# The last group of a second MLP stage by plain products in place of a seven-product scheme

## The chip, the cores and the metric

The kernel runs on one core of a Trainium2 chip. The metric is the device time in microseconds (us) of one execution; lower is better. Inputs and outputs are float32.

## The reference, cut to what matters

The reference is one decoder block: a mixer (dilated attention beside a gated MLP), then a squared-ReLU MLP. The change lies in the second matrix product of that MLP and in the normalisation behind it:

```
h = _rmsnorm(x, norm_pre_mlp)                    # x: (2048, 1024)
a = relu(einsum('bsd,df->bsf', h, w_mlp_in))     # (2048, 4096)
y = einsum('bsf,fd->bsd', a * a, w_mlp_out)      # (2048, 1024)
x = x + _rmsnorm(y, norm_post_mlp)
```

## The kernel before, in words

**Precision.** Every float32 operand of a matmul is split into a high part (a rounded copy made by ScalarE, line L70) and a low part (the source minus the high part, line L78, on VectorE or GpSimd). A product is then three matmuls: high by high, high by low, low by high. Every matmul of this stage takes a 128x128 stationary tile of the squared activations S and a 128x512 moving tile of the weights W2, and adds up in a PSUM bank of 128x512 float32.

**The scheme of the second stage.** The 2048 rows are cut into 16 row tiles of 128, taken two by two: a "block" is a pair of row tiles, `ci` 0 and 1, and there are 8 blocks (two halves of the sequence, `i` = 0 to 3 in each). The 1024 output columns are two halves, `nh` 0 and 1. The inner dimension of 4096 is 32 slices of 128; two slices form a `q`, two `q` a group `g`, so there are 8 groups of four slices. A "step" is one block in one group: 64 steps, numbered `n`, all 8 blocks of group 0 first, then group 1, and so on. The last group is the steps 56 to 63 (`FIRST_END` is 56, `FINAL` is 63).

For a step and a `q`, S is a 2x2 matrix of tiles (row tile by slice) and W2 a 2x2 matrix (slice by column half: B11, B12, B21, B22). The four output tiles need eight tile products done plainly. The kernel uses Winograd's form of Strassen's scheme instead, with seven (`yproduct`, numbered 1 to 7): sums of S tiles and of W2 tiles are formed first (`sum_s` on GpSimd, L1331 to L1334; `sum_w2` and `sum_w2_last` on GpSimd, L1284 to L1292; the sums of weights are named T1 to T4), and several products add to more than one output. Products 1, 6, 7 and 4 grow in one PSUM bank ("ya" in the profile): after each of them VectorE reads the bank and adds it to one output in SBUF (L1537), and only then may TensorE add the next product into the same bank. Product 2 has a bank of its own ("yb"), products 5 and 3 share one ("yc"). So a step has 7 x 2 x 3 = 42 matmuls and seven evictions by VectorE. The output of each step is collected over the groups in SBUF tiles `acc` (the profile shows them under the names of the buffers that they reuse: acc_yt, acc_gmlp, B_acc, acc_y, acc_xr).

**Plain steps.** `plain(n, k)`, with `k` from 0 to 7, does the eight products directly. Output `k // 2` takes two terms, `k` even and `k` odd, side by side in one bank ("y", L1514): B11 and B21 for the left column half, B12 and B22 for the right. VectorE evicts after the second term (L1518). A plain step has 8 x 2 x 3 = 48 matmuls and four evictions. Before the change, three steps are plain: 59, 61 and 63 (the list `PLAIN`). They need B12 as it was, but `sum_w2` has overwritten it in place, so the columns of B12 are loaded again (two DMAs of 256 KB into `w2r_b`) and split again on ScalarE and VectorE.

**Order.** TensorE's order is written out by hand: the list `yorder` sorts all products by a place `t0 + t`, where `t0` grows by 7 with each step. A seven-product step n has its products at 0 (1), 3 (2), 4 (6), 8 (7), 9 (5), 12 (4) and 13 (3), so its last four lie among the first three of step n+1: TensorE does other products while VectorE reads the shared bank. The other engines work in the order of the program text, which follows the same loop; each has one queue, worked off in order. `at(k, gen)` puts a piece of work behind the k-th product of the list. The sums and splits of S for step n+3 (`sum_s`) follow the last product of step n, in pieces; the splits of W2 for the next group (`ops_of`, `op_w2`) follow products 1, 2, 6, 7, 5 and 4 of the last step of a group, when the spot that they overwrite is free, their low parts on GpSimd.

**The end of each output.** In the last group each output is final after its last eviction. `end_half` has ScalarE square and sum it (jk, L1458; the junk goes to a PSUM bank) and GpSimd multiply it by the gain `gfin` (L1465). `finish(n)` then forms the reciprocal root on ScalarE and VectorE (`rstd_act`, L119 to L130), and `end` has VectorE compute y * r + x1 (L1471, four of them for each step) and starts the store (L1472); x1 was loaded by `load_x1` on the SP queue. The last step has its own `finish_row`, which ends its two row tiles apart.

**Banks.** All of these, sums and junk alike, take their PSUM bank from `psum_any`, which alternates between two rings of four banks.

Of the kernel before, what the change touches and what calls it, by code (L numbers as in the profile page):

```python
# [8 lines left out]
F32 = mybir.dt.float32  # L9
# [7 lines left out]
P = 128  # L17
# [24 lines left out]
def block_kernel(ctx, tc, a, out):  # L42
    nc = tc.nc
    pe, act, dve, pool, sp = nc.tensor, nc.scalar, nc.vector, nc.gpsimd, nc.sync
    x = a["x"]

    def stack(es, name, bufs=1, side=None, space=None):
        kw = dict(name=name, bufs=bufs, reuse_waits="tile")
        if side:
            kw["side"] = side  # L50
        if space is not None:
            kw["space"] = space
        return es.enter_context(tc.tile_pool(**kw))
# [10 lines left out]
    def psum_aux(name):  # L64
        return ps.tile([P, 512], F32, name=name, tag="aux")

    def split(hi, lo, src, hi_eng="act", lo_eng="dve"):

        if hi_eng == "act":
            act.activation(hi, src, AF.Copy)  # L70
        elif hi_eng == "pool":
            pool.tensor_scalar(hi, src, 1.0, 1.0, op0=OP.mult, op1=OP.mult)  # L72
        else:
            dve.tensor_copy(hi, src)
        if behind_product is not None and lo_eng == "dve":
            behind_product.append((lo, src, f32(hi)))
        else:
            (pool if lo_eng == "pool" else dve).tensor_sub(lo, src, f32(hi))  # L78
# [231 lines left out]
    with ExitStack() as e1a:  # L310
# [6 lines left out]
        for n in range(2):  # L317
            p = psum_aux(f"busy{n}")
# [27 lines left out]
        blocks = [(c, i) for c in range(4) for i in range(4)]  # L346
        qk = [(g, which) for g in range(3) for which in range(2)]
        for half in range(2):
# [15 lines left out]
            for n, (g, which) in enumerate(qk):  # L364
                w = nxt
# [79 lines left out]
    loaded, late, zps = {}, [], {}  # L445
# [246 lines left out]
    for n in range(len(units) + 1):  # L692
        u = None
        if n < len(units):
            g, c, j = units[n]
# [187 lines left out]
    def psum_any(name):  # L883
        cnt[0] += 1
        return ps.tile([P, 512], F32, name=name, tag="mm" if cnt[0] % 2 else "aux")
# [5 lines left out]
    NQ, LEAD, TRAIL = NF // 2, 5, 3  # L891
# [369 lines left out]
    r4 = stack(e3, "r4", 1, side="right")  # L1261
    OPS = ("B11", "B21", "T2", "T3", "T1", "T4", "B22")
    USE = {1: (0, "B11"), 2: (1, "B21"), 6: (2, "T2"), 7: (3, "T3"), 5: (4, "T1"), 4: (5, "T4"), 3: (6, "B22")}
    w2r_, w2_, st_, n_op, spots = {}, {}, {}, [0], []
# [8 lines left out]
    def op_w2(q, name, lo_eng):  # L1273
        w = spots[n_op[0] % 17]
        n_op[0] += 1
        raw = w2r_[q][:, dict(B11=0, B12=1, B21=2, T2=4, T3=1, T1=0, T4=2, B22=3)[name]]
        split(w[:, 0], w[:, 1], raw, "act", lo_eng)
        w2_[q, name] = w
# [10 lines left out]
    def sum_w2_last(q):  # L1289

        r = w2r_[q]
        pool.tensor_sub(r[:, 2], r[:, 2], r[:, 4])  # L1292

    blocks = [(half, i) for half in (first_half, second_half) for i in range(4)]
    ysteps = [(g, half, i) for g in range(NQ // 2) for half, i in blocks]


    PLAIN = [n for n in range(len(ysteps)) if n >= len(ysteps) - len(blocks) and n % len(blocks) in (3, 5, 7)]
    FINAL = len(ysteps) - 1
    OUTPUTS = [(ci, nh) for ci in range(2) for nh in range(2)]  # L1300

# [12 lines left out]
    def sum_s(n):  # L1314
# [6 lines left out]
        st_[n] = w  # L1321
        if n in PLAIN:
            split(w[:, 0, :, :2], w[:, 1, :, :2], raw[:, :, :2], "act", "dve")
# [16 lines left out]
            yield  # L1340

    def ops_of(g, j, lo_eng="pool"):
        for q in (2 * g, 2 * g + 1):
            op_w2(q, OPS[j], lo_eng)

    last_ones = order[n_last:]

# [6 lines left out]
    q = NQ - 1  # L1354
# [76 lines left out]
    FIRST_END = len(ysteps) - len(blocks)  # L1431
    x1_, ss_, y_, wb_, last_rows = {}, {}, {}, {}, {}
# [18 lines left out]
    def end_half(n, ci, h):  # L1451

        g, half, i = ysteps[n]
        if n not in ss_:
            ss_[n] = sm.tile([P, 2, 2], F32, name=f"fs_{n}", tag="fs")
        y = acc[half, i, ci][:, h * 512:(h + 1) * 512]
        junk = psum_any(f"jk_{n}{ci}{h}")
        act.activation(junk, y, AF.Square, accum_out=ss_[n][:, h, ci:ci + 1])  # L1458
        if n == FINAL and h:

            z = acc[blocks[1] + (ci,)][:, :512]
            dve.tensor_mul(z, y, gfin[h])
            y = z
        else:
            pool.tensor_mul(y, y, gfin[h])  # L1465
        y_[n, ci, h] = y
# [7 lines left out]
    def finish(n):  # L1474

        r_ = rstd_act(sm, ss_[n], 2, 1.0 / D, f"fin{n}")
        r = next(r_)
        yield
        next(r_)
        yield  # L1480
        rows = places_of(n)
        rows = [rows[k] for k in ((0, 1, 2, 3) if n in PLAIN else (0, 3, 2, 1))]
        for k in (0, 2):
            end(n, r, 0, rows[k:k + 2], (sp, sp))
            yield
# [35 lines left out]
    def yproduct(n, i):  # L1521

        g, half, b = ysteps[n]
        j, name = USE[i]
        which = {1: "a", 6: "a", 7: "a", 4: "a", 2: "b", 5: "c", 3: "c"}[i]
        if i in (1, 2, 5):
            ybank[n, which] = psum_any(f"y{which}_{n}")
        p = ybank[n, which]
        for m, q in enumerate((2 * g, 2 * g + 1)):
            s, w = st_[n][:, :, m, S_AT[i]], w2_[q, name]  # L1530
            for o, (l, r) in enumerate(((0, 0), (0, 1), (1, 0))):
                pe.matmul(p, s[:, l], w[:, r], start=i in (1, 2, 5) and not m and not o, stop=m == 1 and o == 2,  # L1532
                          skip_group_check=True)
        ci, nh = {1: (0, 0), 2: (0, 0), 6: (0, 1), 3: (0, 1), 4: (1, 0), 7: (1, 1), 5: (1, 1)}[i]
        an = acc[half, b, ci][:, nh * 512:(nh + 1) * 512]
        if (half, b, ci, nh) in begun:
            dve.tensor_add(an, an, p)  # L1537
        else:
            begun.add((half, b, ci, nh))
            dve.tensor_copy(an, p)  # L1540
        if n >= FIRST_END and i in (2, 5, 4, 3):
            end_half(n, ci, nh)


    yorder, t0 = [], 0
    for n in range(len(ysteps)):
        late = [8, 9, 12, 13]
        if n in PLAIN:
            late = [0] * 8 if n == FINAL else late
            own = [(k, t) for k, t in enumerate([0.5, 2.6, 5.2, 6.2] if n == FINAL else [0, 3, 4, 6.2])]  # L1550
            own += [(k, t) for k, t in enumerate([8, 9, 10, 11] if n == FINAL else late, 4)]
            yorder += [(t0 + t + (0.5 if t >= 7 and n != FINAL else 0), n, ("p", k)) for k, t in own]
        else:
            yorder += [(t0 + t, n, i) for i, t in zip((1, 2, 6, 7, 5, 4, 3), [0, 3, 4] + late)]
        t0 += 7
    yorder.sort(key=lambda z: z[:2])
    def at(k, gen):
# [5 lines left out]
    for k, (_, n, i) in enumerate(yorder):  # L1563
        g = ysteps[n][0]
        nth, more = n % len(blocks), g + 1 < NQ // 2
        if n in PLAIN:
            plain(n, i[1])
        else:
            yproduct(n, i)
        if not n and i in (1, 2):  # L1570
            ops_of(0, 4 + i, "dve")
        if i == 1 and more:
            if nth == 1:
                for w in (2 * g + 2, 2 * g + 3):
                    load_w2(w)
            if nth == 3:
                ops_of(g + 1, 0)
            if nth == 4:
                for part in (0, 1):
                    for w in (2 * g + 2, 2 * g + 3):  # L1580
                        sum_w2(w, part)
        for gen in todo.pop(k, ()):
            next(gen, None)
        if more and nth == len(blocks) - 1 and USE[i][0] < 6:
            ops_of(g + 1, USE[i][0] + 1)
            if i == 1:
                for w in (2 * g + 2, 2 * g + 3):
                    sum_w2_last(w)
        if (n, i) == (FIRST_END - 1, 3):

            for q in (NQ - 2, NQ - 1):
                w2r_[q] = wb_[q % 2] = r4.tile([P, 5, 512], F32, name=f"w2r_b{q}", tag="w2r", bufs=2)
                sp.dma_start(w2r_[q][:, 1], a["w_mlp_out"][2 * q][:, 512:])
        if (n, i) == (FIRST_END + 1, 7):
            for q in (NQ - 2, NQ - 1):
                op_w2(q, "B12", "dve")
        if n >= FIRST_END and i in (2, ("p", 0)):
            load_x1(n)
        if n == FINAL:
            if i[1] == 4:  # L1600
                last_rows[0] = finish_row(0)
            if i[1] in (4, 5, 6):
                next(last_rows[0])
            if i[1] == 7:
                next(finish_row(1))
        elif i in (3, ("p", 7)):
            m = n + 3
            if m < len(ysteps):
                st = sum_s(m)
                next(st)  # L1610
                next(st)
                load_s(m + 1)
                at(k + 6, st)
                at(k + 7, st)
            if not more:
                f = finish(n)
                at(k + 1, f)
                for d in (2, 3, 4) if n == FINAL - 1 else (2, 4, 5):
                    at(k + d, f)
    for k in sorted(todo):  # L1620
        for gen in todo[k]:
# [67 lines left out]
```

## Time and profile before

| | before |
|---|---|
| time, median of 3 runs | 2808.86 us (2806.22 to 2809.36) |
| the profiled execution | 2810.95 us, its span 2809.2 us |
| TensorE busy | 2721.7 us, 97% |
| VectorE busy | 1574.9 us, 56% |
| ScalarE busy | 1062.9 us, 38% |
| GpSimd busy | 979.4 us, 35% |
| mean granted TensorE clock | 0.989 |
| second MLP product, matmuls | 2706 (61 steps of 42, three of 48) |

Busy time counts matmuls that overlap in the pipeline; a matmul of mean 393 ns is started every 228 ns or so. "Idle before" and the waits say how long an engine stood and who released it. The span runs from the first to the last instruction, and the profiled execution's time is 1.75 us more than its span.

### The profile page before, as it was taken

How to read it: one execution, taken by the hardware profiler on the slowest of the kernel's cores; microseconds unless marked ns; L12 is line 12 of the kernel's file. 1: busy time of each engine (PE TensorE's matmuls, PEld its weight loads, DVE VectorE, ACT ScalarE, POOL GpSimd, SP SyncE). 2: the span in 40 equal slices, each digit the busy share in tenths (PEclk: the TensorE clock that was granted, in tenths of full speed). 3: DMA queues.
4: the chain of work that ended last, by engine and by line, in shares of the span. 5: the costliest groups of instructions: out<-in, count | busy, mean ns of one | idle time of the engine just before them, and what ended most of it. 6: DMA issues, size and time to landing. Idle time of an engine off the chain costs nothing.

```text
span 2809.2 us, 36263 instructions
## 1 busy us (share of the span) xinstructions
PE 2721.7 (97%) x13382; PEld 2277.5 (81%) x13382; DVE 1574.9 (56%) x2670; ACT 1062.9 (38%) x2164; POOL 979.4 (35%) x806
## 2 busy tenths in 40 slices
PE   8999999999989999999998999999999999999987
PEld 8889888988878888887787788888887787877765
DVE  5664562433443344555556644655437777777777
ACT  4212111244443322344444555555544323332344
POOL 0251341200000023312215423223224776667775
PEclk9999999999999999999999999999999999999999
DMA  7544446366666554555558433643343222222244
GB/s 248 180 147 165 154 152 191 122 183 199 193 217 191 184 175 136 185 194 158 180 168 280 152 113 120 206 150 115 119 134 98 83 74 66 85 83 83 83 136 171
DMA packets 298673, 426.61 MB, mean 152 GB/s; under 512 B 18560, under 2 KB 172416, under 8 KB 298496
## 3 DMA queue, kind: packets, MB, share of 16 engines
q1 hardware_dynamic: 210800, 373.17, 41.5%
q10 hardware_dynamic: 87696, 51.13, 6.0%
q8 instruction: 105, 1.72, 0.3%
q14 instruction: 72, 0.59, 0.1%
HBM read 283.52 MB, written 140.71 MB: 151 GB/s over the span
## 4 chain that ended last, share of the span: by engine, by line
PE 77%; POOL 8%; DVE 5%; DMA 4%; issue 3%; ACT 2%; SPq 0%; ACTq 0%; DVEq 0%; POOLq 0%
PE ab L994 9%; PE ya L1532 7%; PE ac L994 6%; PE aa L994 5%; POOL T_spots L78 4%; PE g L95 4%; PE g L97 4%; PE g L96 4%; PE yc L1532 3%; PE x L95 3%; PE x L97 3%; PE x L96 3%; PE o L97 2%; PE o L95 2%; PE o L96 2%
## 5 line engine op out<-in xcount | busy, mean ns | idle before, releaser
L1532 PE MATMUL ya<-T_spots,s 128*128 128x512 f32 x1377 | 341.3, 393 | 8.5 <-DVE acc L1540 3.3
L1532 PEld LDWEIGHTS ya<-T_spots,s 128*128 128x128 f32 x1377 | 259.2, 189 | 69.3 <-issue 5.6
L70 ACT ACTIVATE s<-sraw 128x768 fp32r<-128x768 f32 (+1 forms) x189 | 130.2, 700 | 359.3 <-POOL sraw L1332 206.1
L78 DVE TENSOR_TENSOR s<-sraw,s 128x512 fp32r<-128x512 f32 (+1 forms) x181 | 179.0, 1012 | 43.5 <-ACT s L70 43.2
L994 PE MATMUL aa<-B,A 128*128 128x512 f32 x768 | 186.9, 396 | 7.6 <-ACT xs L1008 6.1
L1532 PE MATMUL yc<-T_spots,s 128*128 128x512 f32 x684 | 180.7, 394 | 5.2 <-POOL T_spots L78 5.2
L965 POOL TENSOR_TENSOR s<-w1r 128x512 f32<-128x512 f32 x32 | 43.1, 1348 | 396.2 <-DVE S L78 335.5
L994 PEld LDWEIGHTS aa<-B,A 128*128 128x128 f32 x768 | 145.4, 190 | 41.5 <-ACT xs L1008 6.5
L72 POOL TENSOR_SCALAR w_g<-w_g_r 128x1024 fp32r<-128x1024 f32 x32 | 33.7, 1052 | 410.6 <-PE g L97 323.9
L1532 PEld LDWEIGHTS yc<-T_spots,s 128*128 128x128 f32 x684 | 126.7, 188 | 39.3 <-POOL T_spots L78 13.0
L95 PE MATMUL x<-hT_a,wq 128*128 128x512 f32 x384 | 149.7, 390 | 0.0
L97 PE MATMUL x<-hT_a,wq 128*128 128x512 f32 x384 | 149.4, 389 | 0.0
L96 PE MATMUL x<-hT_a,wq 128*128 128x512 f32 x384 | 149.4, 389 | 0.0
L631 DVE TENSOR_REDUCE o<-po 128x256 f32<-128x512 f32 x48 | 33.2, 691 | 182.6 <-PE po L630 182.6
L78 POOL TENSOR_TENSOR T_spots<-w2r,T_spots 128x512 fp32r<-128x512 f32 x92 | 132.2, 1463 | 0.0
L70 ACT ACTIVATE hl<-r 128x512 fp32r<-128x512 f32 x48 | 30.4, 634 | 231.4 <-POOL r L276 86.7
L95 PE MATMUL g<-hT_b,w_g 128*128 128x512 f32 x256 | 105.6, 412 | 0.0
L95 PE MATMUL o<-wo,mg 128*128 128x512 f32 x256 | 100.9, 394 | 4.6 <-ACT mg L70 4.1
L1331 POOL TENSOR_TENSOR sraw<-sraw 128x256 f32<-128x256 f32 x61 | 45.1, 739 | 172.0 <-DVE s L78 157.7
L95 PE MATMUL g<-hT_a,w_g 128*128 128x512 f32 x256 | 104.5, 408 | 0.0
L793 POOL TENSOR_TENSOR g<-g,g 128x512 f32<-128x512 f32 x28 | 38.8, 1384 | 187.9 <-DVE g L791 185.1
L70 ACT ACTIVATE S<-w1r 128x512 fp32r<-128x512 f32 x96 | 60.2, 631 | 111.9 <-PE ac L994 66.3
(377 smaller groups left out, 7455.7 us busy)
## 6 DMA issues: line engine op xcount, KB each, us to landing
w1r<-in_w_mlp_in_dram SPq DMA_DIRECT2D x64, 512.0 KB, 3.8
sraw<-sd SPq DMA_DIRECT2D x128, 256.0 KB, 3.4
qk<-hl SPq DMA_DIRECT2D x24, 1024.0 KB, 5.3
qq<-qk SPq DMA_DIRECT2D x96, 256.0 KB, 5.0
w_g_r<-in_w_in_dram SPq DMA_DIRECT2D x32, 512.0 KB, 5.3
gated<-gt SPq DMA_DIRECT2D x64, 256.0 KB, 2.8
g<-gated SPq DMA_DIRECT2D x64, 256.0 KB, 4.4
w2r<-in_w_mlp_out_dram SPq DMA_DIRECT2D x16, 1024.0 KB, 7.2
```

The costliest lines, as they stand in the source:

```text
L70: act.activation(hi, src, AF.Copy)
L72: pool.tensor_scalar(hi, src, 1.0, 1.0, op0=OP.mult, op1=OP.mult)
L78: (pool if lo_eng == "pool" else dve).tensor_sub(lo, src, f32(hi))
L95: pe.matmul(ps, lh, rh, start=start, stop=False)
L96: pe.matmul(ps, lh, rl, start=False, stop=False)
L97: pe.matmul(ps, ll, rh, start=False, stop=stop)
L631: dve.tensor_reduce(ot[:, :, j * 64:(j + 1) * 64], po.rearrange("p (b h e) -> p b e h", b=4, h=2), axis=AX.X, op=OP.add)
L793: (dve if dt == KT - 1 else pool).tensor_add(parts[0], parts[0], parts[1])
L965: pool.tensor_add(s1, a21, a22)
L994: pe.matmul(p, w[:, l, k, :], h[:, r, k, :], start=i in (1, 6, 5) and not k and not n, stop=k == 3 and n == 2, skip_group_check=True)
L1331: pool.tensor_add(a22, a21, a22)
L1532: pe.matmul(p, s[:, l], w[:, r], start=i in (1, 2, 5) and not m and not o, stop=m == 1 and o == 2, skip_group_check=True)
```

## The change

All eight steps of the last group become plain. The order of the last group changes: step 56 still shares its first products with the last four of step 55, and from there on each step's eight products stand in one row, 0 to 7, and the next step's follow. For the last group no sums of weights are formed; only the four tiles B11, B21, B12, B22 of each `q` are split (eight splits in place of sixteen), in this order behind the products 1, 2 and 6 of step 55 (B11 much earlier, as before). B12 is no longer overwritten, so its second load and its splits on VectorE go; the `w2r_b` tiles are still made, since x1 is loaded into them. `finish` takes the halves in one order for all steps, and its two pieces of `end` stand behind the fourth and fifth product of the next step for step 62 too (third and fourth before).

```
-    PLAIN = [n for n in range(len(ysteps)) if n >= len(ysteps) - len(blocks) and n % len(blocks) in (3, 5, 7)]
+    PLAIN = range(len(ysteps) - len(blocks), len(ysteps))
+    PLAIN_OPS = ("B11", "B21", "B12", "B22")
...
     def ops_of(g, j, lo_eng="pool"):
+        ops = OPS if g < NQ // 2 - 1 else PLAIN_OPS
         for q in (2 * g, 2 * g + 1):
-            op_w2(q, OPS[j], lo_eng)
+            if j < len(ops):
+                op_w2(q, ops[j], lo_eng)
...
         rows = places_of(n)
-        rows = [rows[k] for k in ((0, 1, 2, 3) if n in PLAIN else (0, 3, 2, 1))]
...
-        if n >= FIRST_END and i in (2, 5, 4, 3):
-            end_half(n, ci, nh)
...
-        late = [8, 9, 12, 13]
-        if n in PLAIN:
-            late = [0] * 8 if n == FINAL else late
-            own = [(k, t) for k, t in enumerate([0.5, 2.6, 5.2, 6.2] if n == FINAL else [0, 3, 4, 6.2])]
-            own += [(k, t) for k, t in enumerate([8, 9, 10, 11] if n == FINAL else late, 4)]
-            yorder += [(t0 + t + (0.5 if t >= 7 and n != FINAL else 0), n, ("p", k)) for k, t in own]
+        if n == PLAIN[0]:
+            yorder += [(t0 + t, n, ("p", k)) for k, t in enumerate((0, 3, 4, 6.2, 7.1, 7.2, 7.3, 7.4))]
+        elif n in PLAIN:
+            yorder += [(t0 + 0.5 + k * 0.8, n, ("p", k)) for k in range(8)]
         else:
-            yorder += [(t0 + t, n, i) for i, t in zip((1, 2, 6, 7, 5, 4, 3), [0, 3, 4] + late)]
+            yorder += [(t0 + t, n, i) for i, t in ((1, 0), (2, 3), (6, 4), (7, 8), (5, 9), (4, 12), (3, 13))]
...
-            if nth == 4:
+            if nth == 4 and g + 1 < NQ // 2 - 1:
                 for part in (0, 1):
                     for w in (2 * g + 2, 2 * g + 3):
                         sum_w2(w, part)
...
-            if i == 1:
+            if i == 1 and g + 1 < NQ // 2 - 1:
                 for w in (2 * g + 2, 2 * g + 3):
                     sum_w2_last(w)
         if (n, i) == (FIRST_END - 1, 3):
-            for q in (NQ - 2, NQ - 1):
-                w2r_[q] = wb_[q % 2] = r4.tile([P, 5, 512], F32, name=f"w2r_b{q}", tag="w2r", bufs=2)
-                sp.dma_start(w2r_[q][:, 1], a["w_mlp_out"][2 * q][:, 512:])
-        if (n, i) == (FIRST_END + 1, 7):
-            for q in (NQ - 2, NQ - 1):
-                op_w2(q, "B12", "dve")
+            for w in range(2):
+                wb_[w] = r4.tile([P, 5, 512], F32, name=f"w2r_b{w}", tag="w2r", bufs=2)
...
-                for d in (2, 3, 4) if n == FINAL - 1 else (2, 4, 5):
+                for d in (2, 4, 5):
                     at(k + d, f)
```

## The prediction

> **What bounds the kernel now.** I read the page first, then the busy time by stretches, then the waits of TensorE in the last group, then the order of time around its longest wait.
>
> The page says which engine to count. Then come three stretches: five steps of group 6 between two starts of product 1; from there, the first matmul of step 56, to the last matmul; and the rest of the span.
>
> ```profile
> PE 2721.7 (97%) x13382; PEld 2277.5 (81%) x13382; DVE 1574.9 (56%) x2670; ACT 1062.9 (38%) x2164; POOL 979.4 (35%) x806
> core 0: us, PE busy (x) PEld busy (x) DVE busy (x) ACT busy (x) POOL busy (x), PEclk, DMA share, GB/s
> 2639.10:2687.03 47.93, 47.93 (x211) 39.43 (x210) 35.65 (x51) 14.88 (x23) 30.32 (x32) 1.00 0.18 56
> 2687.03:2797.94 110.91, 94.88 (x379) 73.06 (x377) 83.94 (x104) 52.32 (x161) 77.72 (x59) 0.95 0.49 166
> 2797.94:2809.20 11.26, 0.00 (x1) 0.00 (x0) 7.84 (x16) 2.42 (x8) 1.57 (x1) 0.69 0.49 186
> ```
>
> TensorE is the bound, and where it isn't held up it is quiet: 5 x 42 = 210 matmuls in 47.93 us, no gap, **0.2282 us each**. In the second stretch lie 378 matmuls: 5 x 42 + 3 x 48 = 354 of the last group, and 24 of step 55 (its last four products). At 0.2282 they need 86.3 us; they take 110.91. So **24.6 us of the last group are lost**. That is the number which decides here. The granted clock is 0.95 against 1.00.
>
> What TensorE waited for in that stretch (total, times, longest):
>
> ```profile
> PE ya L1532 <- DVE acc_yt L1537: 7.1, 4, 3.4
> PE ya L1532 <- DVE B_acc L1537: 4.0, 2, 3.4
> PE yc L1532 <- POOL T_spots L78: 1.6, 3, 0.7
> PE y L1514 <- DVE acc_gmlp L1537: 1.4, 1, 1.4
> PE ya L1532 <- DVE acc_gmlp L1537: 1.4, 1, 1.4
> PE y L1514 <- DVE B_acc L1537: 0.5, 1, 0.5
> ```
>
> Sum 16.0 us. Of these 12.5 (7.1 + 4.0 + 1.4) are products 6, 7 or 4 waiting until VectorE has read the bank that they add to, 1.6 are splits of W2 that GpSimd brings late, 1.9 a plain product behind a bank. The other 8.6 us come after waits. Around one long wait (TensorE's order of time, then two stretches, one with the wait, one without):
>
> ```profile
> 2742.30 1.54 PE L1532 MATMUL yb<-T_spots,s 128*128 128x512 f32 x6
> 2747.27 1.29 PE L1532 MATMUL ya<-spot,s 128*128 128x512 f32 x3 [3.43 <-DVE acc_yt L1537]
> 2748.36 1.48 PE L1532 MATMUL ya<-T_spots,s 128*128 128x512 f32 x3
> 2749.64 4.93 PE L1514 MATMUL y<-T_spots,s 128*128 128x512 f32 x18
> 2790.91 7.03 PE L1514 MATMUL y<-T_spots,s 128*128 128x512 f32 x30
> 2742.30:2755.11 12.81, 8.85 (x31) 6.50 (x29) 9.73 (x14) 6.57 (x21) 6.91 (x5) 0.87 0.30 103
> 2755.11:2769.74 14.63, 14.11 (x60) 11.30 (x61) 11.76 (x13) 6.16 (x20) 9.79 (x9) 1.00 0.79 270
> ```
>
> After 3.43 us of standing, three matmuls take 2748.36 - 2747.27 = 1.09 us and the next three 1.28, where 0.68 is usual; the clock of this stretch is 0.87. The plain product itself runs at the usual pace: 30 in 7.03 us, and 7.03 contains the drain of the last.
>
> Why the bank was read late, in VectorE's order of time between the two:
>
> ```profile
> 2740.69 1.37 DVE L78 TENSOR_TENSOR s<-sraw,s 128x512 fp32r<-128x512 f32 x1 [1.31 <-ACT s L70]
> 2741.99 0.68 DVE L1537 TENSOR_TENSOR acc_yt<-acc_yt,yc 128x512 f32<-128x512 f32 x1
> 2743.97 1.95 DVE L78 TENSOR_TENSOR s<-sraw,s 128x512 fp32r<-128x512 f32 x2 [1.31 <-ACT s L70]
> 2745.85 0.68 DVE L1518 TENSOR_TENSOR acc_yt<-acc_yt,y 128x512 f32<-128x512 f32 x1
> 2746.44 0.68 DVE L1537 TENSOR_TENSOR acc_yt<-acc_yt,ya 128x512 f32<-128x512 f32 x1
> ```
>
> VectorE wasn't short of time; its queue was held: splits of S stood for ScalarE's high part, which stood behind the squares (L1458) of outputs that VectorE had yet to evict. Behind them waited the eviction of ya, and behind that TensorE, which has only one product, 1.37 us, between the two uses.
>
> **The change, part by part.**
>
> Matmuls: 8 x 48 - 354 = 30 more, 30 x 0.2282 = **+6.8 us**.
>
> Waits on the shared bank: a plain output fills its own bank with 12 matmuls, 2.74 us, and nothing is added after the read. Each output takes one bank for sums and one for junk, so the sums stay in one ring of four, and a bank returns after four outputs. VectorE may be late by three outputs, 8.2 us, where it had 1.37; its longest hold here cost 3.43. So these waits, the 1.9 us of plain products and the slow matmuls behind them go.
>
> W2: GpSimd loses eight sums and eight of sixteen splits (two of the sixteen were VectorE's), and they were late:
>
> ```profile
> 2685.57 3.01 POOL L1292 TENSOR_TENSOR w2r<-w2r 128x512 f32<-128x512 f32 x2
> 2705.67 2.53 POOL L78 TENSOR_TENSOR T_spots<-w2r,T_spots 128x512 fp32r<-128x512 f32 x2
> 2682.45 1.99 ACT L70 ACTIVATE T_spots<-w2r 128x512 fp32r<-128x512 f32 x3 [2.37 <-PE yb L1532]
> ```
>
> The last split came at 2705.67, when TensorE stood for it. After the change B12 and B22 follow ScalarE at 2682.45 without the sums; four splits at 1.27 us (2.53 / 2) are done by about 2689, while product 3 of step 56, the first to use B22, starts at 2687.03 + 7 x 1.37 = 2696.6. The 1.6 us go. The two reloads of B12 and their splits on VectorE leave the SP and VectorE queues; nothing that TensorE waits for at length stands behind them: 0.
>
> S: a plain step needs one split on VectorE and one on GpSimd in place of three on VectorE and four sums on GpSimd. The second piece stands behind a product two steps early, so nobody waits for it: 0. Squares, gains, `finish` and x1 loads stay four to a step.
>
> If all goes, the stretch is (384 + 24) x 0.2282 = 93.1 us, **-17.8**. Some waits may remain at the turn from group 6. Nearest row: all of group 6 with its own turn:
>
> ```profile
> 2608.29:2687.03 78.74, 77.67 (x337) 62.77 (x336) 58.99 (x81) 24.48 (x38) 56.28 (x55) 1.00 0.25 81
> ```
>
> 336 matmuls in 78.74 us, 2.1 above 76.7. That turn has 14 splits and four to six sums on GpSimd, mine six splits, so I take 0.5 (between 0 and 2.1): **-17.3**.
>
> Of the 8.6 us of slow matmuls the Trainium skill, "TensorE: Matmul & The Clock Gate", Part 1, says that an idle window of about 3.4 us halves the clock until another is busy, which costs about half a window, 1.7 us. The three waits of 2.6 us and more would then be worth an estimated 5.1 us, and by that rule the sum would be 16.0 + 5.1 - 6.8 = 14.3 us, less than by the rows; the clock of 0.87 agrees in kind, and the rows decide.
>
> The tail. VectorE's last lines, then a square on ScalarE and the first and last line of a root's second half:
>
> ```profile
> 2797.61 0.74 DVE L1471 SCALAR_TENSOR_TENSOR acc_y<-acc_y,r_fin,acc_yt 128x512 f32<-128x512 f32 x1
> 2798.99 1.75 DVE L1471 SCALAR_TENSOR_TENSOR B_acc<-B_acc,r_fin,acc_yt 128x512 f32<-128x512 f32 x1
> 2800.66 0.74 DVE L1471 SCALAR_TENSOR_TENSOR acc_y<-acc_y,r_fin,acc_yt 128x512 f32<-128x512 f32 x1
> 2801.33 0.74 DVE L1471 SCALAR_TENSOR_TENSOR acc_yt<-acc_yt,r_fin,acc_yt 128x512 f32<-128x512 f32 x1
> 2801.99 0.68 DVE L1518 TENSOR_TENSOR acc_xr<-acc_xr,y 128x512 f32<-128x512 f32 x1
> 2797.84 0.58 ACT L1458 ACTIVATE jk<-acc_xr 128x512 f32<-128x512 f32 x1
> 2798.46 0.20 ACT L126 ACTIVATE t_fin<-r_fin 128x1 f32<-128x1 f32 x1
> 2799.11 0.29 ACT L130 ACTIVATE r_fin<-r_fin,t_fin 128x1 f32<-128x1 f32 x1
> ```
>
> The last eviction begins 4.05 us after TensorE's end, behind `finish` of step 62 and the first row tile of step 63; 7.2 us follow that stay. Now step 62 ends eight products before the end (five before), and its L1471 lines stand behind products 3 and 4 of step 63, not 5 and 6. I count VectorE backwards from TensorE's end E: eviction and gain of output 1 to E - 4.1; four L1471 of 0.74 to E - 1.2; eviction 2, ScalarE's square and what follows it up to the root, 2799.40 - 2797.84 = 1.6 us, to E + 1.1; two L1471 to E + 2.6, then the last eviction. 4.05 - 2.6 = 1.4, say **-1.3**. Bounds: 0, if they take 1.75 us as one above, and -3.0, if the last eviction has only the root chain ahead of it (E + 1).
>
> Sum: -17.3 - 1.3 = **-18.6 us**. The profiled execution goes from 2810.95 to 2792.4, span 2790.6; it lies 2.1 above the median of 2808.86, from which I get **2790.3**.
>
> **The rivals.**
>
> (a) VectorE becomes tight. Rows of the last group:
>
> ```profile
> L78 DVE TENSOR_TENSOR s<-sraw,s 128x512 fp32r<-128x512 f32 x13 | 14.6, 1143 | 11.7 <-ACT s L70 11.7
> L1471 DVE SCALAR_TENSOR_TENSOR acc_yt<-acc_yt,r_fin,acc 128x512 f32<-128x512 f32 x4 | 5.7, 1484 | 0.0
> L1465 POOL TENSOR_TENSOR B_acc<-B_acc,gfin 128x512 f32<-128x512 f32 x8 | 12.1, 1518 | 7.9 <-ACT jk L1458 7.9
> ```
>
> A step is 48 x 0.2282 = 10.95 us. In it VectorE has four evictions of 0.68, a split of 1.14 that stands 1.4 us for ScalarE, and four L1471: at 0.74 together 8.2 us, at 1.48 11.2, at 1.75 12.3. With the longest it falls back 1.3 us a step; over steps 56 to 60, which have splits, 6.6 us, still under the slack of 8.2, but TensorE may stand once or twice, and the tail gains nothing. Price 4 to 8 us: about 2796. The Trainium skill, "SBUF — State Buffer", section "SBUF: two separate sides", speaks for it: VectorE with two SBUF inputs and GpSimd exclude each other for a whole instruction. The rows agree (0.74 alone, 1.75 beside GpSimd).
>
> (b) The other side: VectorE's hold per step passes what a step gives, and the ring of four is always full. Each step then takes as long as the worst stretch:
>
> ```profile
> 2713.01:2727.95 14.94, 11.80 (x43) 8.72 (x42) 13.02 (x16) 5.80 (x19) 7.82 (x5) 0.89 0.46 159
> ```
>
> VectorE is 13.02 of 14.94 us busy there, and a step of the last group took about that. Eight steps of 14.94 and 24 x 0.2282 give 125.0 against 110.91: +14.1, 2823. It turns at (110.91 - 5.5) / 8 = 13.2 us per step. Against it: that stretch has splits that a plain step lacks, and the sum in (a) reaches 12.3 at the most.
>
> (c) The change doesn't do what it says at the turn: splits of B21, B12 or B22 come late as in group 6, two or three waits of 0.7 us and one that slows the clock, some 4 us: 2794. Against it: about 6 us between split and use.
>
> **How the numbers follow.** Forecast 0.68, (a) 0.17, (c) 0.09, (b) 0.06. The forecast's own bounds: -17.8 - 3.0 = -20.8 and the lowest run's 2.6 under the median give 2785.5; residual waits of 2.1 and no gain in the tail, -15.7, give 2793. The range reaches past (c) and (a), whose dearer end is 2790.3 + 8 = 2798, to 2799; only (b) and a little more lie outside. A measurement here tells 0.2%, 5.6 us, from no change: faster holds all but (b) and a tenth of (a) gone further: 0.91, same 0.03, slower 0.06.
>
> **What would show it.** Right: from the first y of step 56 to the last matmul about 93 us with 408 matmuls and a clock of 1.00; no wait of TensorE above 0.7 us after the turn; L1292 and its like gone from about 2650 to 2700; the last L1518 at most 3 us after TensorE's end. Wrong: y (L1514) waiting for VectorE's L1518 lines in steps 57 to 63, the clock below 0.97, L1471 at 1.5 us and more throughout, or W2 splits ending behind 2696.

## The result, and the profile after

| | before | after | forecast |
|---|---|---|---|
| time, median of 6 runs | 2808.99 us (2806.22 to 2810.66) | 2792.03 us (2787.64 to 2792.71) | 2790.3 |
| ratio to before, 95% interval | | 0.9938 (0.9925 to 0.9950) | 0.9934 |
| span of the profiled execution | 2809.2 us | 2789.3 us | 2790.6 |
| start of step 56 to TensorE's end | 110.91 us | 93.28 us | 93.6 |
| from there to the end of the span | 11.26 us | 9.81 us | 10.0 |

17 us came off. The interval of the ratio, -14 to -21 us, holds the 18.6 that were forecast. The last two rows carry it, 19.1 us of the two spans. The other 0.8 us came off before any edit reaches: step 56 starts at 2687.03 and at 2686.21 us, but the five steps of group 6 ahead of it take the same time (47.93 and 47.96 us), and the first sum that the change removes stood at 2654.31 us.

The busy time by stretches, after (columns as before): five steps of group 6, the last group, the tail.

```profile
2638.25:2686.21 47.96, 47.96 (x212) 39.44 (x211) 33.21 (x50) 14.13 (x22) 22.52 (x25) 1.00 0.17 56
2686.21:2779.49 93.28, 93.28 (x409) 76.43 (x407) 58.37 (x80) 45.53 (x151) 51.69 (x37) 1.00 0.60 202
2779.49:2789.30 9.81, 0.00 (x0) 0.00 (x0) 5.33 (x12) 1.76 (x6) 1.26 (x1) 0.70 0.31 115
```

408 matmuls in 93.28 us are 0.2286 us each, the quiet pace; the granted clock went from 0.95 to 1.00, and TensorE is busy for the whole stretch. From 2600 us on its waits are two, both of the turn from group 5 to 6, which the change leaves as it was:

```profile
PE yc L1534 <- POOL T_spots L78: 0.7, 1, 0.7
PE ya L1534 <- DVE acc_yt L1539: 0.4, 1, 0.4
```

GpSimd at the turn to the last group, in order of time:

```profile
2671.92 0.73 POOL L1335 TENSOR_TENSOR sraw<-sraw 128x256 f32<-128x256 f32 x1
2678.07 3.07 POOL L78 TENSOR_TENSOR T_spots<-w2r,T_spots 128x512 fp32r<-128x512 f32 x2 [5.41 <-ACT T_spots L70]
2681.09 1.30 POOL L78 TENSOR_TENSOR spot<-w2r,spot 128x512 fp32r<-128x512 f32 x1
2682.35 3.82 POOL L78 TENSOR_TENSOR T_spots<-w2r,T_spots 128x512 fp32r<-128x512 f32 x3
```

GpSimd now stands idle for 5.41 us ahead of its first split, and the last ends at 2686.2, 9.6 us before product 3 of step 56 (2695.77) uses it. In step 59, one half of TensorE's order and VectorE's four evictions:

```profile
2727.93 4.97 PE L1516 MATMUL y<-T_spots,s 128*128 128x512 f32 x21
2728.11 0.68 DVE L1520 TENSOR_TENSOR acc_yt<-acc_yt,y 128x512 f32<-128x512 f32 x1
2730.19 0.69 DVE L1520 TENSOR_TENSOR acc_yt<-acc_yt,y 128x512 f32<-128x512 f32 x1 [1.34 <-PE y L1516]
2734.49 0.68 DVE L1520 TENSOR_TENSOR acc_yt<-acc_yt,y 128x512 f32<-128x512 f32 x1
2735.69 0.69 DVE L1520 TENSOR_TENSOR acc_yt<-acc_yt,y 128x512 f32<-128x512 f32 x1 [0.52 <-PE y L1516]
```

The outputs are whole at about 2727.25, 2729.99, 2732.74 and 2735.48 (every 2.74 us). The evictions end 1.5, 0.9, 2.4 and 0.9 us later. VectorE is still held up, but nobody waits for it.

### The profile page after: what moved, and what is told of

It is laid out like the page before. It is cut to its first block, busy times and chain, and to the rows that moved or that the text cites. A ratio compares the mean times of both kernels' runs of the same rounds, so it can differ in the third digit from the quotient of the medians.

```text
span 2789.3 us, 36260 instructions
## 1 busy us (share of the span) xinstructions
PE 2720.9 (98%) x13412; PEld 2282.3 (82%) x13412; DVE 1545.3 (55%) x2643; ACT 1053.1 (38%) x2151; POOL 945.3 (34%) x777
## 5 line engine op out<-in xcount | busy, mean ns | idle before, releaser
L1534 PE MATMUL ya<-T_spots,s 128*128 128x512 f32 x1272 | 313.3, 392 | 4.7 <-DVE acc L1542 2.7
L1534 PEld LDWEIGHTS ya<-T_spots,s 128*128 128x128 f32 x1272 | 239.1, 188 | 59.1 <-issue 4.5
L78 DVE TENSOR_TENSOR s<-sraw,s 128x512 fp32r<-128x512 f32 x171 | 163.7, 980 | 34.8 <-ACT s L70 33.2
L1534 PE MATMUL yc<-T_spots,s 128*128 128x512 f32 x624 | 164.3, 394 | 3.6 <-POOL T_spots L78 3.6
L1534 PEld LDWEIGHTS yc<-T_spots,s 128*128 128x128 f32 x624 | 115.9, 188 | 33.7 <-POOL T_spots L78 9.7
L78 POOL TENSOR_TENSOR T_spots<-w2r,T_spots 128x512 fp32r<-128x512 f32 x86 | 123.2, 1458 | 5.4 <-ACT T_spots L70 5.4
L95 PE MATMUL g<-hT_a,w_g 128*128 128x512 f32 x256 | 104.5, 408 | 0.0
L97 PE MATMUL g<-hT_a,w_g 128*128 128x512 f32 x256 | 100.8, 394 | 0.0
```

What stands on the lines that cost most here:

```text
L95: pe.matmul(ps, lh, rh, start=start, stop=False)
L97: pe.matmul(ps, ll, rh, start=False, stop=stop)
```

## The experiments

The theory: TensorE met a bank that VectorE had yet to read; a plain output in its own bank doesn't. Rivals: the weights' sums and splits that are gone, the two terms side by side, the new order, VectorE's fewer evictions. Times move by some microseconds from run to run. In the profiled executions that kept the earlier groups as they were, step 56 starts anywhere between 2682 and 2689 us; so each run is read from the start of step 56 to TensorE's end too (the stretch), which is steady. Each ratio is to the kernel before as it was timed beside that run (medians of 2809 to 2810 us).

| run | time, us | ratio to before (95%) | stretch, us |
|---|---|---|---|
| before | 2808.99 | | 110.91 |
| after | 2792.03 | 0.9938 (0.9925 to 0.9950) | 93.28 |
| one bank | 2826.35 | 1.0062 (1.0047 to 1.0077) | 129.98 |
| two banks | 2792.50 | 0.9940 (0.9925 to 0.9954) | 93.40 |
| terms apart | 2791.01 | 0.9938 (0.9921 to 0.9954) | 93.28 |
| sums kept | 2794.20 | 0.9943 (0.9926 to 0.9960) | 93.28 |
| before, no squares | 2800.77 | 0.9968 (0.9956 to 0.9980) | 101.67 |
| a third of the matmuls out | 2781.75 | 0.9904 (0.9890 to 0.9917) | 82.40 |
| six plain steps, old order | 2799.75 | 0.9964 (0.9952 to 0.9975) | 99.74 |
| the same, B12 split earlier | 2798.91 | 0.9957 (0.9943 to 0.9970) | 99.31 |
| two late places mended | 2830.17 | 1.0078 (1.0065 to 1.0090) | 93.28 |
| after, once more | 2789.84 | 0.9927 (0.9915 to 0.9940) | 93.28 |

**One bank, two banks.** The 32 outputs take R banks in turn; the junk of the squares takes the other ring.

```
-            ybank[n, k // 2] = psum_any(f"y{k // 2}_{n}")
+            j = (n - FIRST_END) * 4 + k // 2
+            if j < R:
+                yring.append(ps.tile([P, 512], F32, name=f"yr{j}", tag="aux"))
+            ybank[n, k // 2] = yring[j % R]
```

R = 1: 

> All 32 outputs of the last group take one PSUM bank in turn; everything else is as after the change. Theory (the gain comes from TensorE no longer meeting a bank that VectorE has yet to read): each output now waits for the eviction of the one before, which in the trace after the change ends 0.9 to 2.4 us behind the output (four of step 59: 1.5, 0.9, 2.4, 0.9). 31 waits of 0.9 to 1.5 us: 28 to 46 us lost, 2820 to 2838, slower than before the change, with the same matmuls and the same splits. Rival (the gain comes from the W2 sums and splits that GpSimd is rid of, or from VectorE's fewer evictions): both stay gone, so less than half of the gain is lost, below 2802.

R = 2: 

> The same with two banks in turn. Theory: an eviction may now be late by one output, 2.74 us less its own 0.7, where the latest in the trace after the change ended 2.4 us behind its output; TensorE should wait in all 0 to 3 us: 2792 to 2795. So one output of slack is enough and the ring of four is not what gives the gain. Rival: the slack of three outputs (8.2 us) is needed, as the prediction's working would have it; then several waits of 1 to 2 us in each step, 2800 or more.

With one bank TensorE's waits from 2600 us on, and the stretch, are

```profile
PE yr L1520 <- DVE acc_yt L1524: 10.8, 12, 1.2
PE yr L1520 <- DVE B_acc L1524: 7.4, 8, 1.2
PE yr L1520 <- DVE acc_y L1524: 3.7, 4, 1.2
PE yr L1520 <- DVE acc L1524: 3.4, 4, 0.9
PE yr L1520 <- DVE acc_gmlp L1524: 2.0, 2, 1.2
PE yr L1520 <- DVE acc_xr L1524: 0.9, 1, 0.9
2685.95:2815.93 129.98, 101.80 (x409) 73.99 (x407) 60.02 (x82) 46.50 (x153) 51.41 (x38) 1.00 0.42 146
```

31 waits, 28.2 us. All the work that the change removed is still removed, and the kernel is slower than before the change. With two banks there is no wait and the stretch is 93.40. So one output of slack, 2.74 us, against a latest eviction of 2.4 us, is the whole difference between the two, and at 36.6 us it is worth more than the change itself. One number comes free: 129.98 - 93.28 - 28.2 = 8.5 us over 31 waits, at a clock of 1.00: on average **each wait costs 0.27 us more than it shows**.

**Terms apart.**

```
+            yorder += [(t0 + 0.5 + o * 0.8, n, ("p", k)) for o, k in enumerate(range(8) if n == FINAL else (0, 2, 4, 6, 1, 3, 5, 7))]
```

> Steps 56 to 62 do the first terms of all four outputs and then the second terms, so four banks are open at once; step 63 stays as it is. Theory: a bank returns three products (4.1 us) after its output is whole, more than the 2.4 us by which the latest eviction ended, so TensorE waits 0 to 3 us: 2791 to 2796. Rival (side by side is what removes the waits): evictions come in a bunch of four in 5.5 us, the next step's first terms stand behind them, 5 us or more lost: above 2797.

No wait, 93.28 us. Side by side has no part in the gain: with four banks open at once a bank returns three products after its output is whole, which is enough too.

**Sums kept.** `sum_w2` and `sum_w2_last` run for the last group too (one of them writes over B11 in place of B12), and three unused splits of each `q` follow the four used ones.

```
+    PLAIN_OPS = ("B11", "B21", "B12", "B22", "T2", "T1", "T4")
...
+            pool.tensor_sub(r[:, 0 if q >= NQ - 2 else 1], r[:, 3], r[:, 1])
```

> After the change, but the eight sums of weights and six splits that nobody uses are put back at their old places on GpSimd and ScalarE, behind the ones that are needed. Theory: GpSimd is late only for what is used last, and here nobody waits for that: 0 to 1.5 us more, 2792 to 2793.5. Rival (the weights' work on GpSimd was the cost): waits of TensorE for T_spots come back, and the squares' gains behind them on GpSimd hold finish up: 4 us or more, 2796 and above.

```profile
2682.27:2775.55 93.28, 93.28 (x409) 76.43 (x407) 59.43 (x80) 48.93 (x157) 62.55 (x45) 1.00 0.58 202
```

GpSimd is busy for 62.55 us in place of 51.69, the stretch is the same, and the last split that is used (B22) ends at 2685.2, 6.6 us before its use at 2691.83. The time, 2794.20, lies 0.7 us above the expected range; the four runs spread from 2787.06 to 2796.25. Leaving out the sums saves no time by itself; the six-plain kernels below show what it is good for.

**Before, without squares.** The 32 squares are left out; a small memset on GpSimd sets the sums of squares to one, so the normalisation is missing.

```
-        junk = psum_any(f"jk_{n}{ci}{h}")
-        act.activation(junk, y, AF.Square, accum_out=ss_[n][:, h, ci:ci + 1])
+        cnt[0] += 1
```

> The kernel before the change, with the 32 squares of the last group (L1458) left out; the sums of squares are set to one, so the normalisation is left out and the time alone counts. Theory (the shared bank was read late because VectorE's queue stood in a ring: its splits of S waited for ScalarE's high parts, those stood behind squares, the squares behind evictions that were behind the splits): without squares VectorE's waits for ScalarE fall, and TensorE's waits for evictions go from 14.4 us to 5 or less, the stretch of the last group from 110.9 to about 96, the time to about 2795. Rival (VectorE has too much to do there, 84 us of 111, or GpSimd is what holds it): waits of 10 us and more stay, 2803 to 2808.

```profile
PE ya L1532 <- DVE acc_yt L1537: 6.3, 3, 2.7
PE ya L1532 <- DVE r_fin L125: 2.0, 2, 1.1
PE yc L1532 <- POOL T_spots L78: 1.7, 3, 0.7
PE yc L1532 <- DVE acc_yt L1537: 1.3, 1, 1.3
PE ya L1532 <- DVE B_acc L1537: 1.0, 1, 1.0
2686.80:2788.47 101.67, 89.38 (x379) 69.94 (x377) 84.40 (x103) 32.39 (x100) 81.17 (x68) 1.00 0.52 181
```

Neither side was right: the time, 2800.77, lies between them. Waits for VectorE fall from 14.4 to 10.6 us, not to 5 (the rival's 10 us and more stay), though VectorE's for ScalarE's S parts halve (15.3 us in the last group before, 7.5 now). The single waits tell more than the sum:

```profile
2709.54 0.63 ACT L70 ACTIVATE s<-sraw 128x512 fp32r<-128x512 f32 x1 [10.10 <-POOL sraw L1332]
2716.96 0.93 PE L1532 MATMUL ya<-spot,s 128*128 128x512 f32 x3 [2.69 <-DVE acc_yt L1537]
2741.95 0.94 PE L1532 MATMUL ya<-spot,s 128*128 128x512 f32 x3 [1.09 <-DVE r_fin L125]
2750.08 1.66 PE L1532 MATMUL ya<-T_spots,s 128*128 128x512 f32 x6 [2.38 <-DVE acc_yt L1537]
```

The ring through the squares made the two waits of 3.43 us: the same products now wait for 1.09 and 0.94. The wait of 2.61 us in step 58 stays (2.69). There ScalarE's part of S stands for the sums of S on GpSimd, which come behind GpSimd's late splits of W2, and VectorE's split and eviction stand behind that. And a wait of 0.54 us grows to 2.38, with VectorE busy ahead of it at L1471 lines of up to 1.78 us. So the hold before the change had at least three sources, and GpSimd's work on the weights was one of them. The stretch falls by 9.2 us: 3.7 of waits, and the rest mostly because the matmuls behind the waits keep their pace here (clock 1.00).

**A third of the matmuls left out.** The low-by-high product is missing in the last group, 32 matmuls to a step.

```
-            for o, (l, r) in enumerate(((0, 0), (0, 1), (1, 0))):
+            for o, (l, r) in enumerate(((0, 0), (0, 1))):
```

> After the change, with the low-by-high matmul left out in the last group: 128 fewer, 32 to a step, so that TensorE alone would need 7.3 us for a step and the others become visible. The output is less exact. Theory (VectorE's price of a plain step is its busy 7.7 us of the trace after plus 1.3 us in which a split stands for ScalarE, 9.0 us in steps with a split and about 6.5 without): steps 57 to 60 take 8 to 9 us, TensorE waits for banks there 4 to 8 us in all, and of 29.2 us some 21 to 27 are gained: 2765 to 2771. Rival (a) of the prediction (VectorE needs 11 to 12.6 us): steps of 10.9 us as before, nearly nothing gained, 2784 and above. If TensorE alone counts: 2763.

Three stretches of 32 matmuls each, then VectorE in the second of them, with the line of ScalarE that ends its second stand:

```profile
2718.21:2729.10 10.89, 9.17 (x32) 7.10 (x33) 7.87 (x11) 5.81 (x21) 6.83 (x5) 0.84 0.69 247
2729.10:2740.00 10.90, 7.83 (x32) 5.85 (x33) 7.88 (x11) 5.81 (x21) 6.82 (x5) 1.00 0.68 245
2740.00:2750.89 10.89, 9.14 (x32) 7.11 (x33) 7.88 (x11) 5.81 (x21) 6.83 (x5) 0.85 0.59 202
2731.40 1.48 DVE L78 TENSOR_TENSOR s<-sraw,s 128x512 fp32r<-128x512 f32 x1 [1.85 <-ACT s L70]
2734.94 0.46 ACT L130 ACTIVATE r_fin<-r_fin,t_fin 128x1 f32<-128x1 f32 x2
2735.31 3.95 DVE L1474 SCALAR_TENSOR_TENSOR acc_yt<-acc_yt,r_fin,acc 128x512 f32<-128x512 f32 x4 [1.17 <-DMA sraw<-sd]
```

Of 29.2 us the stretch gained only 10.9; the time, 2781.75, lies between the theory's range and the rival's. A step takes 10.9 us with a third less for TensorE to do, and TensorE waits 11.9 us for VectorE, not 4 to 8. VectorE is busy for 7.88 us of a step and stands 1.85 + 1.17 us for ScalarE's part of S and for the step's root: 7.88 + 3.0 = 10.9. (For the second stand the row names a DMA; the root's last line, L130 on ScalarE, ran just ahead of it.) My theory of 9.0 missed that second stand; rival (a) was nearer. In the steps with a split of S the plain step after the change, 10.95 us of TensorE, is as long as VectorE's queue at its tightest: TensorE is the bound by a hair.

**Six plain steps in the old order.**

```
-    PLAIN = [n for n in range(len(ysteps)) if n >= len(ysteps) - len(blocks) and n % len(blocks) in (3, 5, 7)]
+    PLAIN = [n for n in range(len(ysteps)) if n >= len(ysteps) - len(blocks) and n % len(blocks) >= 2]
```

> The kernel before the change with six plain steps in place of three, 58 to 63; 56 and 57 keep seven products, the sums of weights and the second load of B12 stay, and so does the order with steps laid into each other. 18 more matmuls, 4.1 us. Theory: the waits on the shared bank from step 58 on go, 13 of the 16 us and the slow matmuls behind them, only the 1.6 us behind GpSimd's splits stay: 2789 to 2794, as the change itself, with 12 matmuls fewer. Rival (the new order of the last group is what helps): 2798 and above.

And with one more line, meant to mend that kernel's 4.1 us wait (the move is by five products; the expectation counts seven):

```
-        if (n, i) == (FIRST_END + 1, 7):
+        if (n, i) == (FIRST_END + 1, 2):
```

> As the kernel with six plain steps (58 to 63; sums of weights, reload of B12 and the old order kept), but ScalarE and VectorE split the reloaded B12 behind product 2 of step 57 and not behind product 7 of step 57, seven products earlier. That kernel lost one wait of 4.1 us for this split, a slow clock behind it, and some 2 us in the tail. Theory (only waits on what VectorE or a split brings late count; the order and the sums do not): the 4.1 us wait and the 2 us of slow matmuls go: 2792 to 2795, the change's time within its run-to-run spread. Rival (something else in the old order costs 6 us): 2798 to 2800 again.

The waits in the one (of the SP queue for GpSimd's splits, a load of S behind the reload, ScalarE, TensorE), then ScalarE's and TensorE's in the other:

```profile
SPq L1593 <- POOL T_spots L78: 15.6, 2, 14.8
2708.85 0.86 SPq L1312 DMA_DIRECT2D sraw<-sd  x2
2714.87 0.63 ACT L70 ACTIVATE s<-sraw 128x512 fp32r<-128x512 f32 x1 [4.15 <-DMA sraw<-sd]
2718.77 3.23 PE L1514 MATMUL y<-T_spots,s 128*128 128x512 f32 x6 [4.11 <-ACT T_spots L70]
2711.02 0.63 ACT L70 ACTIVATE T_spots<-w2r_b 128x512 fp32r<-128x512 f32 x1 [4.32 <-DMA w2r_b<-in_w_mlp_out_dram]
2715.05 2.93 PE L1532 MATMUL ya<-T_spots,s 128*128 128x512 f32 x6 [3.38 <-DVE acc_yt L1537]
2726.13 61.79 PE L1514 MATMUL y<-T_spots,s 128*128 128x512 f32 x270
```

The bank waits behave as the theory says: once the steps are plain, 270 matmuls run without a gap, in the old interleaved order too. The times missed it by 6 and 4 us and lie where the rivals had them, though the trace shows another cause in the stretch. The sums overwrite B12, and its reload can start only when GpSimd's last splits have read the buffer: the SP queue stands for them until 2707.18, and step 58 wants the split at 2714.66. Split late, ScalarE stands 4.15 us for a load of S that was issued behind the reload, the split of B12 comes behind that, and TensorE waits 4.1 us; split early, ScalarE stands 4.3 us for the reload itself, VectorE behind ScalarE, and TensorE 3.4 us behind VectorE. Leaving out the sums spares the change all this: B12 stays where it is. (Six plain steps without a reload were not run.) In the tail the rival has a part: it is 12.0 us in both, 2 us longer than the change's, with the last two steps still laid into each other.

**Two late places mended.**

```
-            if i == 1 and g + 1 < NQ // 2 - 1:
+            if i == 7 and g + 1 < NQ // 2 - 1:
                 for w in (2 * g + 2, 2 * g + 3):
                     sum_w2_last(w)
...
+                next(last_rows[0])
-            if i[1] in (4, 5, 6):
+            if i[1] in (4, 5):
                 next(last_rows[0])
```

> After the change with two edits on places where its trace still shows something late. One: the second half of the root of step 63's first row tile follows product 4, not 5, so its L1474 lines follow product 5: the last eviction should begin 0.7 to 1.2 us after TensorE's end and not 2.4, -1.2 to -1.7 us. Two: the last sum of weights of a group (3 us on GpSimd) is formed behind the splits of T2, T3 and T1, not ahead of them: the waits of product 5 for T1, 0.7 us at each of six turns, 4.3 us in the stage, should go. Theory: 2785 to 2788. Rival: T4 and B22 come late in their stead and products 4 and 3 wait, 2790 to 2793.

Neither: 38 us lost, all ahead of step 56 (the stretch is 93.28). The rival named the right late piece, T4, at a far too low price. TensorE's waits in the whole second stage, then the first turn between groups:

```profile
PE ya L1534 <- DVE acc_yt L1539: 33.3, 6, 5.6
2226.23 2.56 POOL L1292 TENSOR_TENSOR w2r<-w2r 128x512 f32<-128x512 f32 x2
2227.56 0.63 ACT L70 ACTIVATE T_spots<-w2r 128x512 fp32r<-128x512 f32 x1 [9.27 <-POOL w2r L1292]
2229.36 0.62 ACT L70 ACTIVATE s<-sraw 128x512 fp32r<-128x512 f32 x1
2230.08 1.75 DVE L78 TENSOR_TENSOR s<-sraw,s 128x512 fp32r<-128x512 f32 x1 [5.59 <-POOL T_spots L78]
2236.19 4.69 PE L1534 MATMUL ya<-T_spots,s 128*128 128x512 f32 x12 [5.57 <-DVE acc_yt L1539]
```

The 0.7 us waits for T1 did go. But the high part of T4 on ScalarE now waits 9.27 us for the late sum; the parts of S stand behind it in ScalarE's queue, VectorE's split of S behind them (its row names GpSimd, but ScalarE's part, begun at 2229.36, was done last), the eviction of ya behind that, and TensorE stands 5.6 us at each of six turns. Behind the first of these waits 12 matmuls take 4.52 us in place of 2.74 (the next product starts at 2240.71), and this too is part of the 38. Those 3 us of GpSimd stood at the right place. In the tail the last eviction began 2.1 us after TensorE's end, not 2.4: no gain worth having, since one L1474 beside GpSimd took 1.75 us.

**After, once more.** 

> The kernel after the change once more, on the same chip as the six-plain kernel, so that the two can be set side by side: 2790 to 2794, 0.4 to 0.8% under the kernel before; TensorE without a wait in the last group.

2789.84 us, 0.9927 (0.9915 to 0.9940), no wait of TensorE in the last group; on the same chip the six-plain kernel took 2798.91. No version that computes the whole product beat the change by more than the spread of its runs.

## Why the prediction was right

**Which loss decides (24.6 us).** Right: all of it went. The stretch was forecast at 93.1 + 0.5 us and measured 93.28.

**How the 24.6 are made up.** 16.0 us of waits were in the rows; the 8.6 us behind them I left whole. The one-bank run splits them: 12 waits at 0.27 us are 3.3, and 5.3 remain. They lie behind the three long waits, of which the first is

```profile
2717.17 1.62 PE L1532 MATMUL ya<-spot,s 128*128 128x512 f32 x3 [2.61 <-DVE acc_yt L1537]
2718.59 3.04 PE L1532 MATMUL ya<-T_spots,s 128*128 128x512 f32 x9
2721.51 1.66 PE L1532 MATMUL yc<-T_spots,s 128*128 128x512 f32 x6
```

Here 12 matmuls take 4.34 us in place of 2.74, 1.6 us more; behind the two waits of 3.43 us, shown for one in the prediction, the first six matmuls lose 1.0 and 1.1 us and the next 18 another 0.65 and 0.5: 4.9 us for the three. The run without squares agrees: 86.3 + 12.3 of waits + 10 x 0.27 = 101.3, measured 101.67 at a clock of 1.00. The rule of the Trainium skill, "TensorE: Matmul & The Clock Gate", Part 1, gave an estimate of 5.1 us for the slow clock. The trace agrees with that part (4.9 us), though one of the three waits, 2.61 us, was shorter than the rule's window; the 3.3 us that the waits cost beyond their length are what it does not contain.

**Matmuls (+6.8).** Right: 408 at 0.2286 us; no dearer in rows of plain products.

**The shared bank (-17.8 with everything behind it).** Right in mechanism, shown by one bank against two. My ground for it, a slack of three outputs, was far more than is needed; one is enough. That VectorE stood in a ring through the squares explains the two waits of 3.43 us, not the one of 2.61.

**W2 (-1.6).** The waits went. But the reason given, less work for GpSimd, is not what is needed: with all sums and splits kept the stretch is the same, since what is used comes first. And the splits had cost more than 1.6 us before: the wait of 2.61 us in step 58 goes back to them as well, by way of the sums of S, which a plain step does not need.

**S, x1, reload: 0.** Right in the trace after; the six-plain runs show that the reload isn't free in every order, by what stands behind it in the SP queue too.

**The tail (-1.3).** Measured 11.26 - 9.81 = 1.45. VectorE's last lines, with TensorE's and the end of the root on ScalarE:

```profile
2777.27 2.22 PE L1516 MATMUL y<-T_spots,s 128*128 128x512 f32 x9
2780.00 0.29 ACT L130 ACTIVATE r_fin<-r_fin,t_fin 128x1 f32<-128x1 f32 x1
2780.39 0.96 DVE L1474 SCALAR_TENSOR_TENSOR acc_y<-acc_y,r_fin,acc_yt 128x512 f32<-128x512 f32 x1 [1.62 <-issue]
2781.27 0.74 DVE L1474 SCALAR_TENSOR_TENSOR acc_yt<-acc_yt,r_fin,acc_yt 128x512 f32<-128x512 f32 x1
2781.93 0.68 DVE L1520 TENSOR_TENSOR acc_xr<-acc_xr,y 128x512 f32<-128x512 f32 x1
```

The last eviction begins 2.44 us after TensorE's end (2779.49); counted backwards I had 2.6, for the reason given: the root of the first row tile stands behind the square of output 2 on ScalarE, and VectorE starts L1474 as it is done (the row itself names no releaser).

**The rivals.** (a) was nearly so: 10.9 us of VectorE's queue against 10.95 of TensorE, but within the slack, so it cost nothing. Its ground was another: not L1471 lines (L1474 now) of 1.5 us and more, since four of them take 3.8 us after the change, but 3.0 us of standing for ScalarE. (b) and (c) didn't come.

## What to carry to other kernels

Count what an engine loses in a stage (its time there less its instructions at the quiet pace) before weighing a scheme with fewer instructions: here 30 more matmuls cost 6.8 us and freed 24.6. Where TensorE fills one bank after another, give it a second one before anything else: one output of slack was worth 37 us in a stretch of 93. (A second bank for the shared sums of the seven-product scheme was not run.) A wait in one queue is passed on through every queue in which something stands behind it; before moving work later, follow who waits for it, and who stands behind that.

## What the runs showed of the hardware

In the one-bank run a wait of TensorE cost 0.27 us beyond its length on average, and 31 waits of up to 1.2 us left the granted clock at 1.00. Longer waits were sometimes followed by slow matmuls. In the run with a third of the matmuls out, the 10.9 us that follow waits of 2.52 and 2.46 us had a clock of 0.84 and 0.85, and the 10.9 us that follow one of 1.72 had 1.00. Before the change, 12 matmuls behind a wait of 2.61 us took 4.34 us in place of 2.74; yet in the run without squares the same product waited 2.69 us, another 2.38, and the clock stayed at 1.00 over the stretch. What tells these apart stays open.
